# Hybrid mLSTM and attention layer: the mLSTM head norms as steps of their own, and the tanh of the merge gates inside the merge

## The chip, the cores and the metric

The kernel runs on one core of one Trainium2 chip. The metric is the time of one execution in microseconds (us) on the device; lower is better. TensorE (PE in the profile) does the matmuls, VectorE (DVE) and ScalarE (ACT) the elementwise work, GpSimd (POOL) small fills, and SyncE (SP) issues most of the DMA transfers. Each engine works through its own queue strictly in the order in which its instructions stand there.

## The reference, cut to what matters

One layer on a sequence of 512 tokens, width 1024, in float32. Two token mixers, each with four heads of 128 channels, work on the same normed input; each head is normed, and both are merged by gates:

```python
hm = mlstm_chunkwise(heads(mq_c), heads(mk_c), heads(mv), i_pre, f_pre)
hm = head_rmsnorm(hm, m_norm_g)                    # per head, over its 128 channels
ya = (sigmoid(mo) * hm) @ w_br_m

hd = diff_attention(q1, q2, k1, k2, heads(dv), lam, rel_bias)
hd = head_rmsnorm(hd, da_norm_g) * (1.0 - lam_init)
yb = hd @ w_br_d

g_a, g_b = split(gates)
x = x + (sigmoid(g_a) * ya + sigmoid(g_b) * yb) @ w_out
```

Behind it come a gated convolutional feed-forward part (1024 to 2 x 2816 and back), a per-layer embedding and a last norm. The change touches neither the mixers' matmuls nor anything behind the merge.

## The kernel before

Activations lie with channels on the 128 partitions and the 512 tokens in the free dimension. Every large product is taken as three matmuls of high and low parts (`mm3`, L95 to L99: high x high, low x high, high x low), each 128x512. A weight block of 128x1024 is loaded by `wload` (L101) into `raw`, and split on ACT (`whi`, L89) and DVE (`wlo`, L90); there are two buffers each. Projections accumulate in PSUM tiles of the tag `mm`, of which there are four; `sc` and `acc` have two each.

The string ORDER (L50 to L53) is the order in which the code of the mixers is written out. `mq`, `mk`, `dq`, `dk`, `ga`, `gb` are projections, `m0` to `m3` the four mLSTM heads (`mlstm`, L424), `M0` to `M3` their ends (`mlstm_end`, L447), `a0` to `a3` the attention heads (`attention`, L464) and `A0` to `A3` their ends (`attention_end`, L496). A scheduler of the language then sorts the instructions of each engine, by priorities and by its own idea of when operands are ready, so that projections fill the time in which a head waits for ACT and DVE.

What the steps are made of:

- An mLSTM head's sums `num` and `den` grow in PSUM by four blocks. For each, a row `rb` is loaded, taken through Exp on ACT, masked on POOL, multiplied with the scores on DVE (L435) and split (`pph`, `ppl`).
- `mlstm_end` loads a row `em`, and calls `head_norm` (L407). That scales `num` into `y` (L410), squares it into `v` (L412), splits `v` (`csph`, `cspl`), sums it over the partitions with two matmuls into a tile `hm0ss` and so on, and takes the root through `rsqrt_of` (L151): Ln, Exp and Square on ACT (L156 to L158), two operations on DVE (L159, L160), then `y` times `r` (L421). The result is multiplied by the output gate `mo` (L458; its tanh is L444) and split into `hmh` and `hml` (L92, L93).
- `attention_end` calls the same `head_norm` on its sum `av`, with tiles named `hd0ss` and so on, and splits into `hdh` and `hdl`.
- `gate` (L502) is a projection, a multiplication by the token norm `rB` on DVE (L506) and a tanh on ACT (L507). Eight of the sixteen gates stand in ORDER, the others in the merge.
- The merge (L549 to L561) goes over eight chunks of 128 channels. A chunk projects all four `hm` into `ya` and all four `hd` into `yb` (two PSUM tiles of `mm`, 12 matmuls each), multiplies each by its gate (L556, L557), adds them and splits them into `mxh` and `mxl`.

ACT evaluates functions from a loaded table. Ln and Exp of the norms, tanh, and gelu need different tables, and a table load (ACT_TABLE_LOAD) stands wherever the next function isn't in the one that is loaded. `rsqrt_of` is given `before=last`, so that its load is issued right behind the cast of `csph`.

Of the kernel before, what the change touches and what calls it, by code (L numbers as in the profile page):

```python
# [16 lines left out]
P = 128  # L17
# [7 lines left out]
EPS = 1e-6  # L25
# [23 lines left out]

ORDER = """  # L50
bias0 if0 mq0 mk0 mq1 mk1 ct0 m0 m1 mk3 mq2 dk0 M0 M1 mk2 m2 mq3 M2 m3 dq0 dv0 M3 a0 dk1 dq1
A0 a1 A1 dk2 dq2 ga3 dq3 a2 A2 ga0 ga2 gb1 dk3 a3 gb3 gb2 gb0 ga1 A3
"""  # L53


# [1 line left out]
def trunk_kernel(ctx, tc, xT, pT, par, oneh, relb, lamv, w_if, w_in, w_v, w_br, w_out, w_up,  # L57
# [12 lines left out]
    def rt(tag, name):  # L70
        return big.tile([P, S], F32R, tag=tag, name=name, bufs=NBUF[tag])

    def tt(tag, name, n=S):
        w = S + 4 if tag == "ev" else S
        return tp.tile([P, w], F32, tag=tag, name=name, bufs=TBUF[tag])[:, :n]
# [7 lines left out]
    def f(ap):  # L83
        return ap.bitcast(F32)


    def split(hi, lo, src, scale=None):
        if scale is None:
            nc.scalar.copy(hi, src)  # L89
            nc.vector.tensor_sub(lo, src, f(hi))  # L90
        else:
            nc.scalar.activation(hi, src, AF.Copy, scale=scale)  # L92
            nc.vector.scalar_tensor_tensor(lo, src, scale, f(hi), op0=ALU.mult, op1=ALU.subtract)  # L93
# [7 lines left out]
    def wload(src, n=1024):  # L101
        raw = wp.tile([P, 1024], F32, tag="raw", name="raw", bufs=2)
        hi = wp.tile([P, 1024], F32R, tag="whi", name="whi", bufs=2)
        lo = wp.tile([P, 1024], F32R, tag="wlo", name="wlo", bufs=2)
        with tc.high_priority(offset=180):
            nc.sync.dma_start(raw[:, :n], src)
            split(hi[:, :n], lo[:, :n], raw[:, :n])
        return hi, lo
# [25 lines left out]
    def col(c):  # L134
        return prm[:, c:c + 1]
# [7 lines left out]
    def sumsq_add(acc, src, first):  # L143
        if first:
            nc.scalar.activation(acc, src, AF.Square)
        else:
            q = tt("hn", "sq")
            nc.scalar.activation(q, src, AF.Square)
            nc.vector.tensor_add(acc, acc, q)

    def rsqrt_of(r, v, a, before=None):  # L151

        if before is not None:
            with tc.issue_after(before.ins):
                nc.scalar.preload_act_table_set("natural_log_exp_and_others")
        nc.scalar.activation(r, v, AF.Ln, scale=2.0 ** -LN_SHIFT)  # L156
        nc.scalar.activation(r, r, AF.Exp, scale=-0.5, bias=lnb)
        nc.scalar.activation(a, r, AF.Square)  # L158
        nc.vector.scalar_tensor_tensor(a, v, -0.5, a, op0=ALU.mult, op1=ALU.mult)  # L159
        nc.vector.scalar_tensor_tensor(r, a, 1.5, r, op0=ALU.add, op1=ALU.mult)  # L160

    def colsum(o, src):
        hi, lo = pair("cs")
        last = nc.scalar.copy(hi, src)
        nc.vector.tensor_sub(lo, src, f(hi))
        nc.tensor.matmul(o, lhsT=ones, rhs=hi, start=True, stop=False)
        nc.tensor.matmul(o, lhsT=ones, rhs=lo, start=False, stop=True)
        return last
# [235 lines left out]
            nc.tensor.matmul(o, lhsT=ones, rhs=ph, start=j == 0, stop=False)  # L404
            nc.tensor.matmul(o, lhsT=ones, rhs=pl, start=False, stop=j == NB - 1)

    def head_norm(o, g, name, extra=None):  # L407

        y = tt("hn", "y")
        nc.scalar.activation(y, o, AF.Copy, scale=col(g))  # L410
        v = tt("hn", "v")
        nc.scalar.activation(v, o, AF.Square)  # L412
        ss = ps("sc", name + "ss")
        last = colsum(ss, v)
        if extra is None:
            nc.vector.tensor_scalar(v, ss, 1.0 / P, EPS, op0=ALU.mult, op1=ALU.add)
        else:
            nc.vector.scalar_tensor_tensor(v, ss, 1.0 / P, extra, op0=ALU.mult, op1=ALU.add)
        r = tt("hn", "r")
        rsqrt_of(r, v, ss, last)  # L420
        nc.vector.tensor_mul(y, y, r)  # L421
        return y

    def mlstm(hh):  # L424
        num, den = ps("acc", f"num{hh}"), ps("acc", f"den{hh}")
# [19 lines left out]
        return t  # L445

    def mlstm_end(hh, num, den, t):  # L447
        em = tt("rb", "em")
        nc.sync.dma_start(em, rd[hh, ROW_OFF[4]:].partition_broadcast(P))
        nc.scalar.activation(em, em, AF.Exp)  # L450
        ad = tt("hn", "ad")
        nc.scalar.activation(ad, den, AF.Abs)
        nc.vector.tensor_max(em, ad, em)
        nc.scalar.activation(em, em, AF.Square, scale=EPS ** 0.5)
        y = head_norm(num, C_GM + hh, f"hm{hh}", em)
        if t is None:
            t = out_gate(hh)
        nc.vector.scalar_tensor_tensor(y, t, 1.0, y, op0=ALU.add, op1=ALU.mult)  # L458
        hi, lo = rt("hz", f"hmh{hh}"), rt("hz", f"hml{hh}")
        split(hi, lo, y, 0.5)  # L460
        return hi, lo


# [30 lines left out]
        return o  # L494

    def attention_end(hh, o):  # L496
        y = head_norm(o, C_GD + hh, f"hd{hh}")
        hi, lo = rt("hz", f"hdh{hh}"), rt("hz", f"hdl{hh}")
        split(hi, lo, y, 1.0 - LAM_INIT)
        return hi, lo  # L500

    def gate(c, name):  # L502
        o = ps("mm", name)
        proj(o, win(c), 0, h)
        t = tt("x", name)
        nc.vector.tensor_mul(t, o, rB)  # L506
        nc.scalar.activation(t, t, AF.Tanh, scale=0.5)  # L507
        return t


# [2 lines left out]
    for step in ORDER.split():  # L513
        what, i = step[:-1], int(step[-1])
        if what == "if":
            rd, cols = gates()
        elif what == "ct":
            ct = turn_cols(cols)
        elif what == "mq":
            mq[i] = conv_silu(i, 0.5, f"mq{i}")  # L520
        elif what == "mk":
            mk[i] = conv_silu(4 + i, 0.5 * P ** -0.5, f"mk{i}")
        elif what == "mo":
            mo[i] = out_gate(i)
        elif what == "m":
            sums[i] = mlstm(i)
        elif what == "M":
            hm[i] = mlstm_end(i, *sums[i], mo.get(i))
        elif what == "dv":
            dv = vproj(1, "dv")  # L530
        elif what == "bias":
            bias, nlam = make_bias(), make_nlam()
        elif what == "dq":
            dq[i] = queries(8 + i, f"dq{i}")
        elif what == "dk":
            dk[i] = keys(12 + i, f"dk{i}")
# [12 lines left out]
    for j in range(KD):  # L549
        ta = ga[j] if j in ga else gate(20 + j, "ga")  # L550
        tb = gb[j] if j in gb else gate(28 + j, "gb")
        w = wload(w_br[j])
        oa, ob = ps("mm", "ya"), ps("mm", "yb")
        proj(oa, w, 0, hm)
        proj(ob, w, 4, hd)
        nc.vector.scalar_tensor_tensor(ta, ta, 1.0, oa, op0=ALU.add, op1=ALU.mult)  # L556
        nc.vector.scalar_tensor_tensor(tb, tb, 1.0, ob, op0=ALU.add, op1=ALU.mult)  # L557
        nc.vector.tensor_add(ta, ta, tb)
        hi, lo = rt("v", f"mxh{j}"), rt("v", f"mxl{j}")
        split(hi, lo, ta, 0.5)  # L560
        mixed.append((hi, lo))  # L561
# [290 lines left out]
```

## Time and profile before

| | us |
|---|---|
| median of 3 runs (830.2 to 831.01) | 830.45 |
| the profiled execution, its own time | 831.68 |
| its span, first to last instruction | 830.0 |
| PE busy in the span | 813.1 (98%) |
| DVE busy | 541.2 (65%) |
| ACT busy | 412.5 (50%) |
| POOL busy | 28.9 (3%) |
| mean granted TensorE clock | 0.995 of full speed |

Matmuls overlap: a 128x512 matmul is shown as 0.39 us long while the next starts 0.23 us later, so waits on PE are read from the distance between starts, and from the idle time that a row shows in brackets with the instruction that ended it.

### The profile page before, as it was taken

How to read it: one execution, taken by the hardware profiler on the slowest of the kernel's cores; microseconds unless marked ns; L12 is line 12 of the kernel's file. 1: busy time of each engine (PE TensorE's matmuls, PEld its weight loads, DVE VectorE, ACT ScalarE, POOL GpSimd, SP SyncE). 2: the span in 40 equal slices, each digit the busy share in tenths (PEclk: the TensorE clock that was granted, in tenths of full speed). 3: DMA queues.
4: the chain of work that ended last, by engine and by line, in shares of the span. 5: the costliest groups of instructions: out<-in, count | busy, mean ns of one | idle time of the engine just before them, and what ended most of it. 6: DMA issues, size and time to landing. Idle time of an engine off the chain costs nothing.

```text
span 830.0 us, 9910 instructions
## 1 busy us (share of the span) xinstructions
PE 813.1 (98%) x3665; PEld 666.0 (80%) x3665; DVE 541.2 (65%) x875; ACT 412.5 (50%) x624; POOL 28.9 (3%) x117
## 2 busy tenths in 40 slices
PE   9999999999999999999999999999999999999995
PEld 7777778887878888888788888888888888888884
DVE  7698787699767854456677777777777343343546
ACT  7556877687776433234654444444444432232433
POOL 0111100000000000000000000000000000000000
PEclk9999999999999999999999999999999999999998
DMA  6472333222122233352333222333223323333402
GB/s 223 136 207 96 102 109 109 78 77 71 58 76 77 77 102 102 123 181 92 111 103 102 101 82 97 102 108 120 87 92 101 96 89 99 94 112 96 142 36 77
DMA packets 28425, 85.97 MB, mean 104 GB/s; under 512 B 3462, under 2 KB 5146, under 8 KB 28248
## 3 DMA queue, kind: packets, MB, share of 16 engines
q1 hardware_dynamic: 27256, 81.96, 30.9%
q0 software_dynamic: 832, 3.11, 1.3%
q8 instruction: 29, 0.48, 0.2%
q10 hardware_dynamic: 288, 0.27, 0.1%
q14 instruction: 20, 0.16, 0.1%
HBM read 83.19 MB, written 3.45 MB: 104 GB/s over the span
## 4 chain that ended last, share of the span: by engine, by line
PE 85%; ACT 5%; DMA 4%; DVE 4%; issue 1%; POOL 0%; SPq 0%; POOLq 0%; DVEq 0%; ACTq 0%
PE uv L99 5%; PE wd L98 5%; PE wd L99 5%; PE uv L97 5%; PE uv L98 5%; PE wd L97 5%; PE ug L99 5%; PE ug L97 5%; PE ug L98 5%; PE gb L98 2%; PE gb L97 2%; PE gb L99 2%; PE ga L97 2%; PE ga L99 2%; PE ga L98 2%; PE wo L97 2%
## 5 line engine op out<-in xcount | busy, mean ns | idle before, releaser
L89 ACT CAST whi<-raw 128x1024 fp32r<-128x1024 f32 (+1 forms) x137 | 138.3, 1010 | 206.4 <-issue 73.0
L90 DVE TENSOR_TENSOR wlo<-raw,whi 128x1024 fp32r<-128x1024 f32 (+1 forms) x136 | 159.8, 1176 | 87.2 <-ACT whi L89 85.8
L97 PE MATMUL wd<-gh,whi 128*128 128x512 f32 x176 | 68.5, 389 | 0.0
L98 PE MATMUL wd<-gl,whi 128*128 128x512 f32 x176 | 68.5, 389 | 0.0
L99 PE MATMUL wd<-gh,wlo 128*128 128x512 f32 x176 | 68.5, 389 | 0.0
L588 DVE SCALAR_TENSOR_TENSOR y<-u,prm,y 128x512 f32<-128x512 f32 x88 | 65.6, 749 | 1.5
L89 ACT CAST gh<-y 128x512 fp32r<-128x512 f32 x22 | 13.7, 621 | 55.5 <-DVE y L597 55.5
L583 DVE TENSOR_TENSOR u<-uv,rffn 128x512 f32<-128x512 f32 x22 | 15.2, 692 | 38.2 <-PE uv L99 38.2
L97 PEld LDWEIGHTS wd<-gh,whi 128*128 128x128 f32 x176 | 33.0, 188 | 6.9
L98 PEld LDWEIGHTS wd<-gl,whi 128*128 128x128 f32 x176 | 33.0, 188 | 6.9
L99 PEld LDWEIGHTS wd<-gh,wlo 128*128 128x128 f32 x176 | 33.0, 188 | 6.8
L586 ACT ACTIVATE y<-u,prm 128x512 f32<-128x512 f32 x44 | 35.7, 814 | 0.2
L595 ACT ACTIVATE y<-y 128x512 f32<-128x512 f32 x22 | 13.9, 632 | 38.9 <-DVE y L588 38.9
L97 PE MATMUL wo<-mxh,whi 128*128 128x512 f32 x64 | 24.9, 389 | 0.0
L98 PE MATMUL wo<-mxl,whi 128*128 128x512 f32 x64 | 24.9, 389 | 0.0
L99 PE MATMUL wo<-mxh,wlo 128*128 128x512 f32 x64 | 24.9, 389 | 0.0
L90 DVE TENSOR_TENSOR gl<-y,gh 128x512 fp32r<-128x512 f32 x22 | 15.2, 692 | 14.7 <-ACT gh L89 14.7
L481 ACT ACTIVATE e<-e,mx 128x128 f32<-128x128 f32 (+3 forms) x32 | 17.8, 558 | 7.0 <-DVE mx L480 6.8
L210 DVE SCALAR_TENSOR_TENSOR y<-u,prm,y 128x512 f32<-128x512 f32 x24 | 17.8, 743 | 2.1 <-ACT y L208 2.0
L582 POOL MEMSET u<- 128x2 f32 x44 | 4.3, 99 | 366.6 <-DVE y L588 357.2
L571 DVE TENSOR_TENSOR x<-x,wo 128x512 f32<-128x512 f32 x8 | 5.5, 687 | 17.2 <-PE wo L99 17.2
L477 DVE CUSTOM_DVE_ANT_0 e<-ds,bias 128x128 f32<-128x128 f32 (+3 forms) x32 | 15.1, 482 | 2.3 <-PE ds L473 2.2
(1093 smaller groups left out, 2226.7 us busy)
## 6 DMA issues: line engine op xcount, KB each, us to landing
raw<-in_w_up SPq DMA_DIRECT2D x44, 512.0 KB, 3.3
raw<-in_w_in SPq DMA_DIRECT2D x36, 512.0 KB, 3.4
raw<-in_w_down SPq DMA_DIRECT2D x16, 512.0 KB, 3.6
x<-in_xT SPq DMA_DIRECT2D x16, 256.0 KB, 4.5
raw<-in_w_br SPq DMA_DIRECT2D x8, 512.0 KB, 3.2
raw<-in_w_out SPq DMA_DIRECT2D x8, 512.0 KB, 3.8
raw<-in_w_gate SPq DMA_DIRECT2D x8, 512.0 KB, 3.4
raw<-in_w_down SPq DMA_DIRECT2D x8, 384.0 KB, 3.3
```

Source lines behind the costliest of these rows:

```text
L89: nc.scalar.copy(hi, src)
L90: nc.vector.tensor_sub(lo, src, f(hi))
L97: nc.tensor.matmul(o, lhsT=lh, rhs=rh, start=start, stop=False)
L98: nc.tensor.matmul(o, lhsT=lh, rhs=rl, start=False, stop=False)
L99: nc.tensor.matmul(o, lhsT=ll, rhs=rh, start=False, stop=stop)
L210: nc.vector.scalar_tensor_tensor(y, u[:, i:i + S], col(c0 + i), y, op0=ALU.mult, op1=ALU.add)
L477: nc.vector.tensor_tensor_reduce(out=e, in0=s[:, :n], in1=bias[hh][:, S - n:], scale=0.125, scalar=-3.0e38, op0=ALU.add, op1=ALU.max, accu ...
L481: nc.scalar.activation(e, e, AF.Exp, bias=mx[:, 1:2], accum_out=mx[:, 2:3])
L583: nc.vector.tensor_mul(u[:, 2:514], o, rB)
L586: nc.scalar.activation(y, u[:, 2:514], AF.Identity, scale=col(c0 + 2), bias=col(c0 + 3))
L588: nc.vector.scalar_tensor_tensor(y, u[:, i:i + S], col(c0 + i), y, op0=ALU.mult, op1=ALU.add)
L595: nc.scalar.activation(gt, gt, AF.Gelu_apprx_tanh)
```

## The change

`head_norm` is gone. `mlstm_end` keeps the scaling, the square, the column sum and the multiplication by the output gate, and returns `y` and `v`, which now lie in two buffers of the tag `hz`. What is left, from Ln to the split, becomes a step `mlstm_norm`, written `N0` to `N3` in ORDER, among the attention heads. `rsqrt_of` is called there without `before`; of the attention ends only that of head 0 still passes it. The tanh of all sixteen gates moves from `gate` into the merge, and `tc.issue_after(last_exp.ins)` holds each of them behind the last Exp of the norms, that of A3. `last_exp` is a new variable that `rsqrt_of` sets.

```diff
 ORDER = """
-A0 a1 A1 dk2 dq2 ga3 dq3 a2 A2 ga0 ga2 gb1 dk3 a3 gb3 gb2 gb0 ga1 A3
+A0 a1 N0 A1 dk2 dq2 N1 ga3 dq3 a2 N2 A2 ga0 ga2 gb1 dk3 N3 a3 gb3 gb2 gb0 ga1 A3
 """
...
-    def head_norm(o, g, name, extra=None):
-
-        y = tt("hn", "y")
-        nc.scalar.activation(y, o, AF.Copy, scale=col(g))
-        v = tt("hn", "v")
+    def mean_square(o, v, name):
+
         nc.scalar.activation(v, o, AF.Square)
         ss = ps("sc", name + "ss")
-        last = colsum(ss, v)
...
+        return ss, colsum(ss, v)
...
     def mlstm_end(hh, num, den, t):
...
-        y = head_norm(num, C_GM + hh, f"hm{hh}", em)
+        y, v = f(rt("hz", f"hmy{hh}")), f(rt("hz", f"hmv{hh}"))
+        nc.scalar.activation(y, num, AF.Copy, scale=col(C_GM + hh))
+        ss, _ = mean_square(num, v, f"hm{hh}")
+        nc.vector.scalar_tensor_tensor(v, ss, 1.0 / P, em, op0=ALU.mult, op1=ALU.add)
         if t is None:
             t = out_gate(hh)
         nc.vector.scalar_tensor_tensor(y, t, 1.0, y, op0=ALU.add, op1=ALU.mult)
+        return y, v
+
+    def mlstm_norm(hh, y, v):
+        r, t = tt("hn", "r"), tt("hn", "t")
+        rsqrt_of(r, v, t)
+        nc.vector.tensor_mul(t, y, r)
         hi, lo = rt("hz", f"hmh{hh}"), rt("hz", f"hml{hh}")
-        split(hi, lo, y, 0.5)
+        split(hi, lo, t, 0.5)
         return hi, lo
...
     def attention_end(hh, o):
-        y = head_norm(o, C_GD + hh, f"hd{hh}")
+        y, v, r = tt("hn", "y"), tt("hn", "v"), tt("hn", "r")
+        nc.scalar.activation(y, o, AF.Copy, scale=col(C_GD + hh))
+        ss, last = mean_square(o, v, f"hd{hh}")
+        nc.vector.tensor_scalar(v, ss, 1.0 / P, EPS, op0=ALU.mult, op1=ALU.add)
+        rsqrt_of(r, v, ss, None if hh else last)
+        nc.vector.tensor_mul(y, y, r)
...
     def gate(c, name):
...
         nc.vector.tensor_mul(t, o, rB)
-        nc.scalar.activation(t, t, AF.Tanh, scale=0.5)
         return t
...
     for j in range(KD):
         ta = ga[j] if j in ga else gate(20 + j, "ga")
         tb = gb[j] if j in gb else gate(28 + j, "gb")
+        with tc.issue_after(last_exp.ins):
+            for t in (ta, tb):
+                nc.scalar.activation(t, t, AF.Tanh, scale=0.5)
```

The scheduler then puts the engines' instructions in another order. The first place is the end of attention head 3 on PE, from the last matmul of `av3` to the first of the column sum `hd3ss`. `ga` is the last gate projection, `ya` a chunk of the merge. Before:

```order
L99 MATMUL av3_2523<-aph_2559,dvl3_1539 128x256
L99 MATMUL ga_2670<-h5h_231,wlo_2673 128x512
L97 MATMUL ga_2670<-h6h_255,whi_2672 128x512
L98 MATMUL ga_2670<-h6l_256,whi_2672 128x512
L99 MATMUL ga_2670<-h6h_255,wlo_2673 128x512
L97 MATMUL ga_2670<-h7h_282,whi_2672 128x512
L98 MATMUL ga_2670<-h7l_283,whi_2672 128x512
L99 MATMUL ga_2670<-h7h_282,wlo_2673 128x512
L97 MATMUL ya_2734<-hmh0_985,whi_2729 128x512
L98 MATMUL ya_2734<-hml0_986,whi_2729 128x512
L166 MATMUL hd3ss_2708<-csph_2709,ones_89 128x512
```

The same place on PE in the changed kernel, where `ya_2766` is the second chunk of the merge and whi_2761 its weights:

```order
L99 MATMUL av3_2517<-aph_2553,dvl3_1503 128x256
L99 MATMUL ya_2766<-hmh0_1926,wlo_2762 128x512
L97 MATMUL ya_2766<-hmh1_2045,whi_2761 128x512
L98 MATMUL ya_2766<-hml1_2046,whi_2761 128x512
L99 MATMUL ya_2766<-hmh1_2045,wlo_2762 128x512
L97 MATMUL ya_2766<-hmh2_2254,whi_2761 128x512
L98 MATMUL ya_2766<-hml2_2255,whi_2761 128x512
L99 MATMUL ya_2766<-hmh2_2254,wlo_2762 128x512
L97 MATMUL ya_2766<-hmh3_2433,whi_2761 128x512
L98 MATMUL ya_2766<-hml3_2434,whi_2761 128x512
L169 MATMUL hd3ss_2699<-csph_2700,ones_89 128x512
```

The gate projection and the first chunk now stand ahead of this place. From the last matmul of `av3` to the first that reads `hdh3` there stood 43 matmuls before; there stand 21 now.

The second place is ACT in the same stretch, from the scaling of `av3` to the split of head 3. `r` is the tile of Ln and Exp. Before:

```order
L410 ACTIVATE y_2704<-av3_2523,prm_72 128x512
L412 ACTIVATE v_2706<-av3_2523 128x512
L164 CAST csph_2709<-v_2706 128x512
L89 CAST whi_2768<-raw_2767 128x1024
L507 ACTIVATE ga_2701<-ga_2701 128x512
L155 ACT_TABLE_LOAD
L156 ACTIVATE r_2716<-v_2706 128x512
L157 ACTIVATE r_2716<-r_2716,lnb_91 128x512
L158 ACTIVATE hd3ss_2708<-r_2716 128x512
L92 ACTIVATE hdh3_2724<-y_2704 128x512
```

ACT in the changed kernel, from the last Exp (L160) on; L562 is the tanh of the gates:

```order
L160 ACTIVATE r_2696<-r_2696,lnb_91 128x512
L562 ACT_TABLE_LOAD
L562 ACTIVATE ga_2312<-ga_2312 128x512
L161 ACTIVATE hd3ss_2699<-r_2696 128x512
L562 ACTIVATE gb_2659<-gb_2659 128x512
L562 ACTIVATE ga_2692<-ga_2692 128x512
L562 ACTIVATE gb_2378<-gb_2378 128x512
L562 ACTIVATE ga_2345<-ga_2345 128x512
L562 ACTIVATE gb_2626<-gb_2626 128x512
L562 ACTIVATE ga_2080<-ga_2080 128x512
L92 ACTIVATE hdh3_2713<-y_2694 128x512
```

The table load moved from ahead of Ln to behind Exp, and seven tanh came in between Exp and the split; behind the split stands the eighth.

The third place is ACT in the end of mLSTM head 1, from the cast of `csph` on. Before:

```order
L164 CAST csph_1001<-v_998 128x512
L155 ACT_TABLE_LOAD
L89 CAST whi_1250<-raw_1249 128x1024
L92 ACTIVATE hmh0_985<-y_930 128x512
L156 ACTIVATE r_1008<-v_998 128x512
L444 ACT_TABLE_LOAD
L444 ACTIVATE mo_1047<-mo_1047 128x512
L157 ACTIVATE r_1008<-r_1008,lnb_91 128x512
L208 ACTIVATE y_1089<-u_1086,prm_72 128x512
L158 ACTIVATE hm1ss_1000<-r_1008 128x512
```

The same place in the changed kernel:

```order
L167 CAST csph_989<-hmv1_985 128x512
L215 ACTIVATE u_864<-y_867 128x512
L447 ACTIVATE em_977<-em_977 128x512
L89 CAST whi_1033<-raw_1032 128x1024
L92 ACTIVATE mq2h_874<-y_867 128x512
L436 ACTIVATE mo_973<-mo_973 128x512
L422 ACTIVATE rb_1096<-rb_1096,ct_634 128x384
```

No root and no table load is left there. In the whole program 20 table loads stood on ACT before, and 7 stand there now.

## Rows read from the trace of the kernel before

**Rows 1.** The page's first part: busy time, share of the span, instructions.
```profile
PE 813.1 (98%) x3665; PEld 666.0 (80%) x3665; DVE 541.2 (65%) x875; ACT 412.5 (50%) x624; POOL 28.9 (3%) x117
```

**Rows 2.** Windows: stretch, length, busy time by engine (instructions), granted clock, DMA.
```profile
63.70:67.00 3.30, 3.30 (x10) 2.72 (x10) 3.30 (x6) 0.62 (x1) 0.06 (x1) 0.50 0.00 0
87.00:92.00 5.00, 3.56 (x19) 2.67 (x18) 3.76 (x8) 4.60 (x9) 0.29 (x1) 1.00 0.44 82
100.00:160.00 60.00, 58.93 (x272) 47.90 (x272) 44.62 (x69) 44.80 (x71) 3.94 (x14) 1.00 0.32 103
160.00:276.40 116.40, 116.10 (x550) 93.31 (x550) 95.36 (x251) 86.04 (x163) 3.67 (x15) 1.00 0.22 73
276.40:800.00 523.60, 523.49 (x2315) 432.59 (x2314) 303.82 (x383) 208.11 (x266) 6.21 (x44) 1.00 0.32 103
```

**Rows 3.** PE's waits in all: for whom, us in total, times, longest.
```profile
PE num L97 <- ACT pph L89: 2.5, 4, 1.4
PE s L97 <- ACT mk0h L92: 2.0, 1, 2.0
```

**Rows 4.** Timeline of PE, mLSTM heads: start, length, instruction [idle, who ended it].
```profile
106.17 0.39 PE L98 MATMUL mk<-h6l,whi 128*128 128x512 f32 x1
106.77 0.50 PE L166 MATMUL hm1ss<-csph,ones 128*128 128x512 f32 x1 [0.22 <-ACT csph L164]
...
130.14 0.39 PE L97 MATMUL dvp<-whi,h0h 128*128 128x512 f32 x1
130.99 0.36 PE L97 MATMUL num<-pph,mvh 128*128 128x256 f32 x1 [0.46 <-ACT pph L89]
...
147.04 0.39 PE L99 MATMUL dvp<-whi,h3l 128*128 128x512 f32 x1
147.74 0.35 PE L97 MATMUL num<-pph,mvh 128*128 128x256 f32 x1 [0.31 <-ACT pph L89]
```

**Rows 5.** Groups of ACT by line: table loads, count, busy us, mean ns.
```profile
L155 ACT ACT_TABLE_LOAD x10 | 12.8, 1283 | 0.2
```

**Rows 6.** Timeline of PE, end of attention head 3 and start of the merge.
```profile
267.28 0.28 PE L99 MATMUL av<-aph,dvl 128*128 128x256 f32 x1
...
270.72 0.39 PE L167 MATMUL hd3ss<-cspl,ones 128*128 128x512 f32 x1
...
277.09 0.62 PE L97 MATMUL yb<-hdh,whi 128*128 128x512 f32 x2
```

**Rows 7.** Timeline of ACT in the same stretch.
```profile
267.60 0.69 ACT L410 ACTIVATE y<-av,prm 128x512 f32<-128x512 f32 x1 [1.36 <-PE av L99]
268.18 0.59 ACT L412 ACTIVATE v<-av 128x512 f32<-128x512 f32 x1
268.80 0.62 ACT L164 CAST csph<-v 128x512 fp32r<-128x512 f32 x1
...
270.93 1.28 ACT L155 ACT_TABLE_LOAD   x1
272.27 0.63 ACT L156 ACTIVATE r<-v 128x512 f32<-128x512 f32 x1
272.94 0.72 ACT L157 ACTIVATE r<-r,lnb 128x512 f32<-128x512 f32 x1
273.69 0.60 ACT L158 ACTIVATE hd3ss<-r 128x512 f32<-128x512 f32 x1
276.51 0.63 ACT L92 ACTIVATE hdh<-y 128x512 fp32r<-128x512 f32 x1 [2.21 <-DVE y L421]
```

**Rows 8.** Timeline of DVE in the same stretch.
```profile
271.56 0.68 DVE L416 TENSOR_SCALAR v<-hd3ss 128x512 f32<-128x512 f32 x1
...
274.33 0.70 DVE L159 SCALAR_TENSOR_TENSOR hd3ss<-v,hd3ss 128x512 f32<-128x512 f32 x1 [1.11 <-ACT hd3ss L158]
275.06 0.69 DVE L160 SCALAR_TENSOR_TENSOR r<-hd3ss,r 128x512 f32<-128x512 f32 x1
275.78 0.69 DVE L421 TENSOR_TENSOR y<-y,r 128x512 f32<-128x512 f32 x1
```

More of the change, by code (lines that the diff above doesn't have):

```diff
@@ L149, in sumsq_add @@
             nc.vector.tensor_add(acc, acc, q)
+    last_exp = None
     def rsqrt_of(r, v, a, before=None):
@@ L156, in rsqrt_of @@
         nc.scalar.activation(r, v, AF.Ln, scale=2.0 ** -LN_SHIFT)
-        nc.scalar.activation(r, r, AF.Exp, scale=-0.5, bias=lnb)
+        nonlocal last_exp
+        last_exp = nc.scalar.activation(r, r, AF.Exp, scale=-0.5, bias=lnb)
         nc.scalar.activation(a, r, AF.Square)
@@ L405, in weighted @@
             nc.tensor.matmul(o, lhsT=ones, rhs=pl, start=False, stop=j == NB - 1)
-    def head_norm(o, g, name, extra=None):
-        y = tt("hn", "y")
-        nc.scalar.activation(y, o, AF.Copy, scale=col(g))
-        v = tt("hn", "v")
+    def mean_square(o, v, name):
         nc.scalar.activation(v, o, AF.Square)
         ss = ps("sc", name + "ss")
-        last = colsum(ss, v)
[L415 to L422, printed above, removed]
+        return ss, colsum(ss, v)
     def mlstm(hh):
@@ L528, in trunk_kernel @@
             hm[i] = mlstm_end(i, *sums[i], mo.get(i))
+        elif what == "N":
+            hm[i] = mlstm_norm(i, *hm[i])
         elif what == "dv":
```

## The prediction

> **What bounds the kernel now.** I read the page's first part first: PE is busy 98% of the span, the other engines 65% or less [rows 1]. So the sum is PE's own work plus the stretches in which PE waits, and a change that takes nothing off PE can win only those. The windows say where they are. From 160 us to 276.4 us PE is busy 116.10 of 116.40 us, and behind that 523.49 of 523.60; from 100 us to 160 us, where the mLSTM heads 1 to 3 end, it is 58.93 of 60.00 [rows 2]. The busy time hides small losses, because matmuls overlap, so I took the pace: 2315 matmuls in 523.60 us are 0.226 us each [rows 2]. Against that pace, the distances between starts hold 0.60 - 0.23 = 0.37, 0.85 - 0.23 = 0.62 and 0.70 - 0.23 = 0.47 us of waiting [rows 4]. That is 1.46 us in all, and each time ACT ends the wait. The list of waits shows the rest of what ACT costs: 2.5 us in four waits for `pph`, the longest 1.4 us, and 2.0 us once for `mk0h` [rows 3]. The longest of both kinds lie ahead of the column sum `hm0ss`, and up to there no engine's order is changed. What the change can win is therefore small.
>
> The last thing to read is the handover from attention head 3 to the merge, since ACT's order was changed most there. The last matmul of `av3` starts at 267.28, and the first that reads `hdh3` is the second of the pair at 277.09, so it starts near 277.3 [rows 6]. The chain between them runs over ACT and DVE and ends with the split at 276.51 + 0.63 = 277.14 [rows 7]. PE has 43 other matmuls queued in between, 43 x 0.226 = 9.7 us, and the chain takes 9.86 us from 267.28 on. The two are equal within 0.2 us: PE doesn't wait, but it has nothing to spare.
>
> **What is removed.** A table load takes 1283 ns [rows 5], and the next function starts 1.34 us after the load did (270.93 to 272.27) [rows 7]. 13 of 20 loads go, 13 x 1.34 = 17.4 us of ACT. ACT isn't the bound, so this counts only where PE waits for ACT. In `M1` to `M3` the loads, Ln, Exp, Square and the split of each head leave ACT's queue, and `pph` no longer stands behind them or behind `em`. I take the 1.46 us as won [rows 4].
>
> **What is moved into the attention.** Each `N` step issues four operations on ACT (Ln, Exp, Square, split; 0.60 to 0.72 us) and four on DVE (0.69 us) [rows 7, 8]. Head 3's stood inside the stretch 160 to 276.4 already, so it gets twelve more of each: on DVE 12 x 0.69 = 8.3 us on top of 95.36, 103.7 of 116.4 us or 89% [rows 2]. ACT gets 12 x 0.65 = 7.8 us, and loses six of the eight loads that lay there, 6 x 1.34 = 8.0, so it stays at 86. Both engines have room; the cover is PE's queue of projections. If DVE doesn't keep up, PE waits at the transposes and at `av`, which is a rival below. No transfer is added and SP's queue keeps its kinds of work. But the heads 2 and 3 of the mLSTM now stand closer together on PE, with less projection work between the end of `hm2ss` and the third block of `num3`, whose row waits for the buffer that `em` frees. Such a wait costs between 0 and the longest, 1.4 us [rows 3]; I take 0.8, between the 0.47 us that this place has now [rows 4] and that longest. So the mixers up to `av3` come out at -1.46 + 0.8 = -0.7 us.
>
> **What is moved into the merge.** Here the change adds a wait. The order shows three facts. PE has 21 matmuls, not 43, between the last of `av3` and the first that reads `hdh3`: the last gate and the first merge chunk have been used up earlier, because the attention of the heads 2 and 3, slowed by the `N` steps, stands later among them. Behind these 21 there is nothing else, since the third chunk needs a PSUM tile and a pair of weight buffers of the first one, and the first one needs `hdh3`. And ACT now has a table load and seven tanh between the last Exp and the split that makes `hdh3`.
>
> I walk the chain from the start of the last `av3` matmul, with the lengths of ACT and DVE [rows 7, 8]. As before, `csph` is cast by 268.80 + 0.62 - 267.28 = 2.14 us. Then `cspl` on DVE 0.68 (taken as `v` of DVE) to 2.86, its matmul 0.39 [rows 6] to 3.3, `v` 0.68 to 4.0, Ln 0.67 to its successor, and Exp 0.72 to 5.44. The load takes 1.28, to 6.74. The first tanh starts at 6.76. Operations of ACT that wait for nothing follow each other at 0.58 us (267.60 to 268.18) [rows 7]: Square starts at 7.34, six tanh follow, and the split starts at 7.34 + 7 x 0.58 = 11.40 and ends at 12.03. DVE is done earlier: from Square's end at 7.94 it has three operations of 0.70 and one gate product, until 10.9, so the tanh and not DVE decide. PE has run dry at 0.11 + 21 x 0.226 = 4.86. **PE waits 12.05 - 4.86 = 7.2 us.**
>
> The wait has a tail. The next matmul needs `hdl3`, one DVE operation later (0.69), 0.5 us more than PE's pace. The third chunk's weights share buffers with the first chunk's, so their split can only start when PE has read the first's last block; that adds some 0.4 us for the high part and 0.5 for the low part, by the same rows. At full pace the tail is 1.4 us. The clock makes it longer: behind the 2.0 us wait for `mk0h` [rows 3] the granted clock was 0.50, the lower of its two levels (1.2 of 2.4 GHz), for the 3.3 us of the window 63.70 to 67.00, in which 10 matmuls started [rows 2]. A wait of 7.2 us is longer than that one, so I expect the same behind it. Nine matmuls stand before PE needs the low weights; at half pace they take 9 x 0.43 + 0.3 for `hdl3` = 4.2 us instead of 2.0. The tail is then 2.1 us, and the waits for weights fall into it. The merge start costs 7.2 + 2.1 = **9.3 us**, at least 7.2 + 1.4 = 8.6 if the clock stays up.
>
> **Sum.** 9.3 - 0.7 = 8.6 us. On the profiled execution this is 831.68 + 8.6 = 840.3. That execution lies 1.2 us above the median of the runs, so on the median 830.45 + 8.6 = **839.0 us**. Nothing behind the merge gives it back: from 276.4 to 800 PE has 0.1 us of idle time [rows 2].
>
> **The rivals.** *The ACT queue was what PE waited for, and the handover stays hidden (faster).* Then the relieved ACT gives back those 1.46 us [rows 4] and the 0.30 us of the attention [rows 2], and the `av3` chain fits behind PE's queue: 830.45 - 1.46 - 0.30 = 828.7. It decides where the chain from `av3` to `hdh3` is shorter than 4.86 us. For it speaks that all of these waits end on ACT; against it, that the part of the chain up to the end of Exp is 5.4 us alone, with no tanh in it. 4%. In the Trainium skill, "ScalarE: Activation LUTs", section "What ACT_TABLE_LOAD costs", a switch of tables is put at 1283 ns plus a drain of about 1380 ns, 2.66 us, and the section on table sets advises to batch calls by set. By that rule ACT sheds 13 x 2.66 = 34.6 us, an estimate from the page, and this rival would be the likely one. The trace agrees on the load and not on the drain: Ln started 0.06 us behind the load's end [rows 7]. And the batching is what puts the seven tanh in front of `hdh3`, which the rule doesn't weigh.
>
> *Nothing measurable.* The wait at the merge is there but is only some 1 to 2 us, because PE arrives late from waits that it had anyway: 830.45 +- 1.7. Against it: every such wait would itself add to the time. 4%.
>
> *The wait without its tail.* The clock stays up, and all 1.46 us are won with no new wait: 8.6 - 1.46 = 7.1, or 837.6; with two of the tail's waits gone as well (0.9 us), 836.7. For it: behind the 1.4 us wait [rows 3] the granted clock stayed at 1.00, the window 87 to 92 us [rows 2]. 22%.
>
> *DVE becomes the bound of the attention.* At 89% busy and in strict order, a part of its 8.3 us more comes through to PE at the scores, transposes and `av`. If a third does, 839.0 + 2.8 = 841.8; if half, 843.2. For it: the scheduler moved the scores of the heads 2 and 3 later, as if DVE were full. Against it: PE's waits in 160 to 276.4 are 0.3 us now [rows 2], and where scores stand later, projections stand in front of them as cover. 17%.
>
> **How the numbers follow.** The forecast 839.0 has 53%. With 22% at 836.7 to 837.6 and 17% at 841.8 to 843.2, the range is 834.5 to 843.5 and leaves out the two rivals of 4% and some of the ends. Its low end takes the 7.2 us with only the 0.5 for `hdl3` as tail, all of the 1.46 and 0.30 us won (836.4), 0.1 us less at each of the 14 steps of the walk, and half of the spread of the runs, 0.4. The high end is the fourth rival's 843.2 with the same 0.4. Slower by over 0.2%, about what a measurement of this kernel can tell from no change (1.7 us): 92%. Within it 4%, faster 4%.
>
> **What would show it.** In the profile of the changed kernel, a wait on PE of about 7 us at the first `yb` that reads `hdh`, put down to ACT `hdh` L92, near 275 us. Behind it some 3 us of a granted clock of 0.5, and matmuls 0.43 us apart. On ACT, the row of tanh in front of that split. Between 100 and 160 us PE's waits for `csph` and `pph` of the old places gone, and perhaps one near 0.8 us at the third block of `num3`. From 160 us to `av3`, DVE near 89% with PE still near 100%. I am wrong if PE doesn't wait at `hdh3`, if the wait is much shorter than 7 us, or if waits of more than 2 us appear at `at` or `av`.

## The result and the profile of the changed kernel

The changed kernel takes 840.28 us (median of 4 runs, 839.08 to 841.12), the kernel before 830.73 beside it: a ratio of 1.0108, 95% interval 1.0087 to 1.0129, or 9.5 us more. Forecast were 839.0 us, with a range of 834.5 to 843.5. The span of the profiled execution is 838.9 us (830.0 before), its own time 840.65. One of the runs below, of `norms_early_tanh_behind`, took 1657.06 us, twice its others, and is left out.

First the page's busy line and four windows of the changed kernel (stretch, length, busy time by engine with instructions, granted clock, DMA), which answer to [rows 1] and [rows 2]:

```profile
PE 815.0 (97%) x3665; PEld 666.2 (79%) x3665; DVE 541.4 (65%) x875; ACT 395.1 (47%) x611; POOL 30.9 (4%) x117
```

```profile
100.00:160.00 60.00, 59.05 (x274) 48.17 (x273) 36.70 (x55) 31.48 (x51) 4.02 (x13) 1.00 0.29 101
160.00:276.40 116.40, 116.08 (x550) 92.61 (x549) 98.41 (x257) 76.19 (x156) 3.72 (x15) 1.00 0.21 73
276.40:800.00 523.60, 517.03 (x2269) 426.52 (x2268) 305.44 (x386) 212.62 (x274) 6.21 (x44) 0.99 0.31 103
281.80:291.90 10.10, 6.42 (x14) 4.67 (x15) 7.82 (x12) 6.88 (x11) 0.00 (x0) 0.50 0.15 48
```

ACT is busy 17.4 us less, and the time is 9.5 us longer. The counts on PE say where: from 100 to 160 us it starts 2 matmuls more than before (0.45 us won), from 160 to 276.4 the same 550, and behind that 2269 instead of 2315. These 46 overstate the loss, since some of them, near 800 us, are short. A better measure is the first matmul behind the merge, that of `wo`, ahead of which both kernels have 1583 matmuls. The kernel before:

```profile
357.04 0.39 PE L97 MATMUL wo<-mxh,whi 128*128 128x512 f32 x1
```

and the changed kernel:

```profile
366.31 0.39 PE L97 MATMUL wo<-mxh,whi 128*128 128x512 f32 x1
```

It comes 9.3 us later, although PE was 0.45 us ahead when the merge began, so the start of the merge costs 9.7 us. The last row of the windows, with 14 matmuls in 10 us at half the clock, lies in this stretch. PE's list of waits (for whom, us in total, times, longest) has one new large entry:

```profile
PE yb L97 <- ACT hdh L92: 6.5, 1, 6.5
PE num L97 <- ACT pph L89: 2.7, 4, 1.5
PE s L97 <- ACT mk0h L92: 1.9, 1, 1.9
...
PE rmixss L169 <- ACT csph L167: 1.0, 1, 1.0
```

The timeline of PE around that wait (start, length, instruction, idle time ahead of it) answers to [rows 6]:

```profile
273.77 0.28 PE L99 MATMUL av<-aph,dvl 128*128 128x256 f32 x1
...
278.63 0.39 PE L99 MATMUL yb<-hdh,wlo 128*128 128x512 f32 x1
285.48 0.79 PE L97 MATMUL yb<-hdh,whi 128*128 128x512 f32 x1 [6.46 <-ACT hdh L92]
286.21 0.79 PE L98 MATMUL yb<-hdl,whi 128*128 128x512 f32 x1
286.80 0.63 PE L99 MATMUL yb<-hdh,wlo 128*128 128x512 f32 x1
287.23 0.63 PE L97 MATMUL yb<-hdh,whi 128*128 128x512 f32 x1
```

Between 273.77 and 278.63 PE works off its 21 matmuls, then it has nothing until 285.48: a distance of 6.85 us where 0.23 would be its pace, so 6.6 us. Behind it the starts are 0.43 us apart. ACT (answering to [rows 7]) shows what it does meanwhile:

```profile
277.95 0.63 ACT L158 ACTIVATE r<-v 128x512 f32<-128x512 f32 x1 [2.04 <-DVE v L502]
278.61 0.72 ACT L160 ACTIVATE r<-r,lnb 128x512 f32<-128x512 f32 x1
279.35 1.28 ACT L562 ACT_TABLE_LOAD   x1
280.65 0.63 ACT L562 ACTIVATE ga<-ga 128x512 f32<-128x512 f32 x1
281.18 0.58 ACT L161 ACTIVATE hd3ss<-r 128x512 f32<-128x512 f32 x1
281.70 0.61 ACT L562 ACTIVATE gb<-gb 128x512 f32<-128x512 f32 x1
...
284.30 0.61 ACT L562 ACTIVATE ga<-ga 128x512 f32<-128x512 f32 x1
284.82 0.61 ACT L92 ACTIVATE hdh<-y 128x512 fp32r<-128x512 f32 x1
```

The load and one tanh stand ahead of Square, six more tanh, 0.52 us apart, ahead of the split. DVE (answering to [rows 8]) has its last operation on the way at 283.84:

```profile
283.84 0.68 DVE L504 TENSOR_TENSOR y<-y,r 128x512 f32<-128x512 f32 x1
```

It ends at 284.52, 0.3 us before the split starts: the tanh decide, but by little.

### The profile page after: what moved, and what is told of

It is laid out like the page before. It is cut to its first block, busy times and chain, and to the rows that moved or that the text cites. A ratio compares the mean times of both kernels' runs of the same rounds, so it can differ in the third digit from the quotient of the medians.

```text
span 838.9 us, 9892 instructions
## 1 busy us (share of the span) xinstructions
PE 815.0 (97%) x3665; PEld 666.2 (79%) x3665; DVE 541.4 (65%) x875; ACT 395.1 (47%) x611; POOL 30.9 (4%) x117
## 4 chain that ended last, share of the span: by engine, by line
PE 87%; DVE 4%; DMA 3%; ACT 3%; issue 2%; SPq 0%; POOL 0%; POOLq 0%; DVEq 0%; ACTq 0%
PE wd L99 5%; PE wd L97 5%; PE uv L97 5%; PE uv L98 5%; PE uv L99 5%; PE wd L98 5%; PE ug L98 5%; PE ug L97 5%; PE ug L99 5%; PE ga L97 2%; PE ga L99 2%; PE ga L98 2%; PE gb L99 2%; PE gb L98 2%; PE gb L97 2%
## 5 line engine op out<-in xcount | busy, mean ns | idle before, releaser
L97 PE MATMUL yb<-hdh,whi 128*128 128x512 f32 x32 | 13.4, 418 | 6.5 <-ACT hdh L92 6.5
```

What stands on the lines that cost most here:

```text
L97: nc.tensor.matmul(o, lhsT=lh, rhs=rh, start=start, stop=False)
```

## The experiments

Each kernel is compared with runs of the kernel before taken beside it, whose median was 830.7 to 831.7 us. "Last start" and "first of `hdh3`" are distances on PE from the start of the last `av3` matmul; the wait is that of PE's list. "Matmuls between" are those on PE between the last of `av3` and the first that reads `hdh3`.

| kernel | matmuls between | last start ahead of the wait | first of `hdh3` | wait | median, us |
|---|---|---|---|---|---|
| changed kernel | 21 | 4.87 | 11.72 | 6.5 | 840.28 |
| `tanh_behind_split` | 21 | 4.88 | 9.10 | 3.8 | 838.86 |
| `norm_steps_alone` | 27 | 6.27 | 10.39 | 3.7 | 840.96 |
| `norm3_later` | 29 | 6.73 | 11.73 | 4.6 | 839.61 |
| `dve_load_alone` | 26 | 6.05 | 9.11 | 2.7 | 836.05 |
| `norms_short` | 44 | 10.21 | 11.86 | 1.3 | 833.19 |
| `tanh_move_alone` | 49 | | | none | 832.83 |
| `pe_kept_busy` | 48 | | | none | 837.15 |
| `norms_before_attention` | 55 | | | none | 836.60 |

The fourth column is a chain over ACT and DVE, about 9.1 us without the row of tanh, 11.8 with it, and 10.4 where a load stands ahead of Exp. The third is 0.11 us plus 0.227 for each matmul, within about 0.1 in all six rows. Their difference, less one matmul of 0.23, is the wait within 0.2 us. So the wait has two causes that can be moved one by one: the chain, and the cover on PE, that is, the matmuls it still has to do. In the kernel before the first that reads `hdh3` starts near 277.3 [rows 6], 10.0 us behind `av3`, with 43 matmuls in between and no wait. Of the 6.6 us of the changed kernel, 22 matmuls fewer are 5.0, and the chain, longer by 1.7, is the rest.

### The tanh behind the split of `hdh3`

```diff
-        with tc.issue_after(last_exp.ins):
+        with tc.issue_after(hd3_split.ins):
```

`hd3_split` is the operation on ACT that makes `hdh3`.

> The changed kernel, with the tanh of the merge gates ordered behind the split that makes hdh3 instead of behind the last Exp; PE's order is unchanged, with the same 21 matmuls between av3 and the first that reads hdh3. Theory A (the table load and the seven tanh stand in the chain to hdh3): Square starts 1.83 us earlier (279.35 instead of 281.18 in the trace of the changed kernel), then DVE's three operations of 0.70 us, with or without one gate product between them, decide; the split moves from 284.82 to between 282.0 and 282.7, so the wait at hdh3 falls from 6.5 to between 3.7 and 4.4 us. Some of it comes back, since the load, the tanh and the two weight splits now stand behind hdh3: up to 0.5 us. So 2.1 to 2.8 us less than the changed kernel's 840.3, about 837.5 to 838.2. Theory B (the loss is the lost cover on PE, whatever stands on ACT): as the changed kernel, 840.3. Theory C (the queue of tanh is all of the loss): back to the kernel before, 830.7.

Measured: 838.86 us (836.59 to 839.71), a ratio of 1.0096 (1.0075 to 1.0117). One row of PE's waits and four of ACT:

```profile
PE yb L100 <- ACT hdh L95: 3.8, 1, 3.8
```

```profile
278.80 0.60 ACT L164 ACTIVATE hd3ss<-r 128x512 f32<-128x512 f32 x1
281.61 0.63 ACT L95 ACTIVATE hdh<-y 128x512 fp32r<-128x512 f32 x1 [2.21 <-DVE y L507]
282.26 1.28 ACT L566 ACT_TABLE_LOAD   x1
283.55 0.63 ACT L566 ACTIVATE ga<-ga 128x512 f32<-128x512 f32 x1
```

Without the tanh ACT waits for DVE ahead of the split, and the wait is what theory A gave, 2.7 us shorter. Only 1.4 us of it shows in the median, from runs that lie 3 us apart, and 3.2 us in the spans of the two profiled executions (838.9 and 835.7), so the size of what comes back behind the split isn't settled. The larger part of the loss stays: the tanh row isn't all of it.

### Each half of the change alone

```diff
 A0 a1 A1 dk2 dq2 ga3 dq3 a2 A2 ga0 ga2 gb1 dk3 a3 gb3 gb2 gb0 ga1 A3
...
+        with tc.issue_after(last_exp.ins):
+            for t in (ta, tb):
+                nc.scalar.activation(t, t, AF.Tanh, scale=0.5)
```

> The kernel before with the second half of the change alone: tanh moved into the merge behind the last Exp, norms left at the ends of the mLSTM heads. By the order PE has 49 matmuls between the last of av3 and the first that reads hdh3, and ACT has a load and six tanh ahead of the split. Theory A: PE runs dry at 0.11 + 49 x 0.226 = 11.2 us behind the start of the last av3 matmul. ACT: csph cast until 2.14, load until 3.44, a weight split of 1.05 until 4.5, Ln and Exp until 5.9, load until 7.2, tanh, Square and five tanh at 0.52 us each to 10.8, split until 11.4. The wait is 0.2 to 0.5 us, and the time 830.7 to 831.7. A rival: a load and a row of tanh ahead of the split cost the 6 us that they take on ACT, whatever PE has left to do: 837. Another rival: the moved N steps carry nothing of the loss and this kernel is as slow as the changed one, 840.

Measured: 832.83 us, a ratio of 1.0028 (1.0016 to 1.0041). There is no wait for `hdh3` in PE's list; its largest entries are those of the kernel before:

```profile
PE num L97 <- ACT pph L89: 2.7, 4, 1.6
PE s L97 <- ACT mk0h L92: 1.8, 1, 1.8
```

The row of tanh, behind which PE waited 6.5 us, costs nothing at the handover when 49 matmuls cover it; both rivals fall. The 2.0 us that it is slower lie elsewhere: in its trace PE has lost them when the projection `if` starts, at 32.1 us instead of 30.1. The order of no engine differs up to there.

```diff
         nc.vector.tensor_mul(t, o, rB)
+        nc.scalar.activation(t, t, AF.Tanh, scale=0.5)
         return t
...
-        with tc.issue_after(last_exp.ins):
-            for t in (ta, tb):
-                nc.scalar.activation(t, t, AF.Tanh, scale=0.5)
```

> The changed kernel with the first half of the change alone: the norms as steps of their own in the attention, tanh back in the gates. By the order PE has 27 matmuls between the last of av3 and the first that reads hdh3; no tanh stands between Exp and the split, but a load stands ahead of Ln and another ahead of Exp in every norm (15 loads in all). Theory A: PE runs dry at 0.11 + 27 x 0.226 = 6.2 us. ACT: csph until 2.14, load until 3.44, Ln at 4.0 to 4.7, load to 6.0, Exp to 6.7, Square to 7.3; DVE three operations of 0.70 to 9.4; split to 10.0. The wait is 3.8 us, with a tail of 1.4 to 3 us behind it and 0.7 us won in the mixers: 835.2 to 836.8. Rival: the moved norms are harmless and the tanh row is all of the loss: 830.

Measured: 840.96 us, a ratio of 1.0124 (1.0109 to 1.0139). The wait at `hdh3` is what was expected, but theory A missed the time by 4 us, since new waits on DVE stand in the attention:

```profile
PE yb L97 <- ACT hdh L92: 3.7, 1, 3.7
...
PE at L494 <- DVE mx L479: 1.2, 1, 1.2
PE ds L475 <- DVE mx L479: 0.8, 2, 0.6
PE ds L475 <- DVE r L163: 0.5, 1, 0.5
```

In its trace the last `av3` starts 2.1 us later than in the changed kernel (275.84), although 6 matmuls fewer stand ahead of it: that is 3.4 us. So the N steps alone cost as much as the whole change, and the tanh alone 2.0 us, none of it at the handover. The tanh in the merge take the table loads out of the attention (15 loads here, 7 in the changed kernel) and lengthen the chain at its end; together with the N steps that comes out even.

### PE kept busy through the wait

```diff
+    warm2 = ps("acc", "warm2")
+    with tc.issue_after(last_mm.ins):
+        for i in range(28):
+            nc.tensor.matmul(warm2, lhsT=ones, rhs=hm[0][0], start=i == 0, stop=i == 27)
```

`last_mm` is the second matmul of the column sum of head 3, and nothing reads `warm2`.

> The changed kernel with 28 matmuls of 128x512 added that nothing reads, queued on PE behind the column sum of attention head 3, so that PE works through the wait for hdh3 (48 matmuls in between instead of 20 or 21; 28 x 0.226 = 6.3 us, the length of the wait). In the trace of the changed kernel the granted clock is 0.50 for 10.24 us from inside the wait on, and PE's starts from 260 to 300 us hold 11.3 us beyond its pace, 6.6 of them the wait itself. Theory A (the tail is the clock that fell while PE stood still): the clock stays at 1.00, the matmuls behind hdh3 follow at 0.22 us, the wait shrinks to about 0.7 us, and the time falls by 2 to 3 us to 837.3 to 838.3, although PE has 28 matmuls more to do. Rival (the tail is waits for hdl3 and for weights, which a busy PE doesn't shorten): the same time as the changed kernel, 840.3.

Measured: 837.15 us (836.81 to 837.57), 3.1 us less than the changed kernel, with 28 matmuls more. Two windows, from the added matmuls on:

```profile
278.00:284.00 6.00, 6.00 (x28) 4.74 (x26) 3.88 (x6) 5.99 (x11) 0.00 (x0) 1.00 0.00 0
284.00:300.00 16.00, 15.98 (x70) 12.80 (x69) 13.11 (x19) 6.92 (x9) 0.00 (x0) 1.00 0.30 98
```

The granted clock stays at 1.00 and the matmuls at their pace, and no wait for `hdh` is left in PE's list. What stood behind the wait was the clock, and the weights and `hdl3` cost nothing that can be seen beside it.

### A gate held back as cover

```diff
-                ga[i] = gate(20 + i, "ga")
+            with tc.issue_after(last_av.ins) if ("ga", i) in LATE else nullcontext():
+                ga[i] = gate(20 + i, "ga")
```

`LATE` holds `ga1` alone, and `last_av` is the last matmul of the attention sum.

> The changed kernel with the N steps and the tanh where the change puts them, but the projection of the last gate of the order (ga1, 24 matmuls) held back on PE until behind the last matmul of av3. 62 matmuls then stand between it and the first that reads hdh3, 24 of them ahead of the column sum of head 3. Theory A (cover): PE runs dry at 0.11 + 62 x 0.226 = 14.1 us; the column sum comes only behind 24 matmuls, at 5.5 us, which makes the chain some 2.8 us longer than 11.7: 14.5. The wait is about 0.4 us; if the attention, which has lost 24 matmuls to put between its own, still keeps PE at work, the time is 830.5 to 832. Rival (the attention on DVE is as slow as the order assumes, and the N steps are the bound): PE waits in the attention for what it lost, 24 x 0.226 = 5.4 us, and the time is 836 to 838.

Measured: 844.05 us, a ratio of 1.0149 (1.0123 to 1.0175): slower than the changed kernel, and beyond both theories. PE no longer waits at `hdh3`; it waits in attention head 3. Two rows of its waits and the windows around:

```profile
PE at L501 <- DVE e L495: 2.5, 2, 1.3
PE at L501 <- DVE mx L486: 2.5, 1, 2.5
```

```profile
160.00:260.00 100.00, 99.70 (x472) 79.87 (x471) 87.19 (x227) 69.51 (x142) 3.38 (x13) 1.00 0.22 74
260.00:276.00 16.00, 9.59 (x29) 5.91 (x28) 10.59 (x31) 5.37 (x13) 0.34 (x2) 0.62 0.09 33
```

Between the scores, the transposes and `av` of the last head PE now has nothing to do for 6.4 of 16 us, and the clock falls there instead. The rival has the place and the size of the waits (5.4 us), but not the time, 6 us over its 838; how much of that is the clock, no run parts. The projections are one stock: what is kept for the handover is missing in the attention. The same kernel with the tanh behind the split:

> As gate_behind_av3, and the tanh of the merge ordered behind the split that makes hdh3. 52 matmuls in between: PE runs dry at 11.9 us, the chain of 8.9 with the later column sum ends at 11.7. Theory A: no wait at hdh3 and 829.8 to 831, the same as the kernel before. Rival (DVE is the bound in the attention): waits of up to 5.4 us there, 835.

Measured: 843.16 us (1.0141, 1.012 to 1.0163), with the same waits at the transposes. The rival's waits came in both, its 835 didn't, and my own belief, that the attention has projections to spare, fell.

### The norms ahead of the attention

```diff
-A0 a1 N0 A1 dk2 dq2 N1 ga3 dq3 a2 N2 A2 ga0 ga2 gb1 dk3 N3 a3 gb3 gb2 gb0 ga1 A3
+A0 a1 A1 dk2 dq2 ga3 dq3 a2 A2 ga0 ga2 gb1 dk3 a3 gb3 gb2 gb0 ga1 A3
```

and `N0 N1 N2 N3` stand between `M3` and `a0`.

> The changed kernel with its four N steps moved in the order of steps to one place ahead of attention head 0, so that none of them stands in the attention; tanh stays in the merge, behind the last Exp, as in the changed kernel. By the order 55 matmuls stand on PE between the last of av3 and the first that reads hdh3 (the changed kernel has 21, the one before 43), 17 of them ahead of the column sum. Theory A (the loss is the length of the chain to hdh3 minus PE's cover): PE runs dry at 0.11 + 55 x 0.226 = 12.5 us behind the start of the last av3 matmul; the chain is the changed kernel's 11.7 and about 1.1 more, since the column sum comes only after 17 matmuls (3.95 us), 12.8. The wait is 0 to 0.5 us, and the time 830.5 to 832. Rival (the row of tanh and the load cost what they take on ACT, wherever the norms stand): 837. Rival (norms outside the end of the head cost their time on DVE wherever they stand): 839.

Measured: 836.60 us (1.006, 1.0042 to 1.0077). The wait at `hdh3` is gone, as theory A has it, but the time isn't. Two rows of PE's waits and two of DVE's timeline:

```profile
PE mo L97 <- DVE dvl L296: 2.0, 1, 2.0
...
PE ds L475 <- DVE mx L479: 1.5, 1, 1.5
```

```profile
157.59 0.69 DVE L162 SCALAR_TENSOR_TENSOR t<-hmv,t 128x512 f32<-128x512 f32 x1 [2.35 <-ACT t L161]
...
161.87 2.06 DVE L296 SCALAR_TENSOR_TENSOR dvl<-dvp,rtok,dvh 128x512 fp32r<-128x512 f32 x3
```

The norms now stand on DVE ahead of `dvl`, which frees the PSUM tiles that the output gate's projection needs, and DVE waits there for ACT, which has 15 table loads again, eight of them between 139 and 167 us. The price has moved; the two waits are 3.5 of the 5.7 us over the kernel before. With the tanh behind the split as well:

> As norms_before_attention, and the tanh of the merge ordered behind the split that makes hdh3. 45 matmuls in between: PE runs dry at 0.11 + 45 x 0.226 = 10.3 us; the chain without the tanh row took 8.9 by the walk, with the later column sum 10.0. Theory A: no wait at hdh3, 830 to 831, the same as the kernel before within 0.2%; a gain over the kernel before only if the fewer table loads (15 instead of 20) take something off the waits for pph, at most 1 us. Rival: the weights and the gate products, which now stand behind the tanh, make PE wait in the second and third chunk, 1 to 2 us: 831.5 to 833.

Measured: 836.78 us (835.59 to 837.7; 1.0065, 1.0049 to 1.0081), with the same wait of 2.0 us for `dvl` and none at `hdh3`; theory A and the rival both missed that wait.

### Work on DVE alone, and less of it

```diff
+        elif what == "D":
+            d = tt("hn", "d")
+            nc.vector.tensor_mul(d, rB, rB)
+            for _ in range(3):
+                nc.vector.tensor_mul(d, d, rB)
...
-A0 a1 A1 dk2 dq2 ga3 dq3 a2 A2 ga0 ga2 gb1 dk3 a3 gb3 gb2 gb0 ga1 A3
+A0 a1 D0 A1 dk2 dq2 D1 ga3 dq3 a2 D2 A2 ga0 ga2 gb1 dk3 D3 a3 gb3 gb2 gb0 ga1 A3
```

> The kernel before, unchanged but for sixteen products of 128x512 on DVE that nothing reads, in four steps of four at the places of the attention where the change puts its N steps (0.69 us each, 11 us of DVE). No instruction is added on PE or ACT. The order answers with 26 matmuls between the last of av3 and the first that reads hdh3 instead of 43. Theory A (the attention of the kernel before has no slack on DVE: what is put there uses up PE's stock of projections, and PE stands still at the end of it): PE runs dry at 0.11 + 26 x 0.226 = 6.0 us, the chain to hdh3 is the 9.9 us of the kernel before, the wait 3.9 us, with a tail of 2 to 3 us at the lower clock: 836.5 to 838. Rival (DVE, busy 95 of 116 us there, has room for it): 830.7.

Measured: 836.05 us (1.0056, 1.0035 to 1.0076), 4.4 us over the kernel before, with no edit on ACT or PE. A row of PE's waits and the window behind it:

```profile
PE yb L97 <- ACT hdh L92: 2.7, 1, 2.7
```

```profile
282.80:286.10 3.30, 3.03 (x7) 2.03 (x8) 1.45 (x3) 1.56 (x3) 0.00 (x0) 0.50 0.00 0
```

The chain was 0.8 us shorter than I had taken it, and PE ran dry 0.3 us later. The rival falls: with DVE busy 95 of 116 us there [rows 2], 11 us more weren't free, though a part fitted in: from 160 to 268 us DVE is busy 97.7 us, 89.6 before. And the 26 matmuls come from the scheduler's order, which is made ahead of the run by its own idea of DVE; whether DVE itself would have let `av3` come earlier, this run doesn't tell.

```diff
-        rsqrt_of(r, v, t)
+        nc.scalar.activation(r, v, AF.Ln, scale=2.0 ** -LN_SHIFT)
+        nc.scalar.activation(r, r, AF.Exp, scale=-0.5, bias=lnb)
         nc.vector.tensor_mul(t, y, r)
```

> The changed kernel with a shorter N step: the Square on ACT and the two operations on DVE that refine the inverse root of the mLSTM heads are left out, so that a head's step has two operations on DVE instead of four (8 x 0.69 = 5.5 us less on DVE in the attention). The heads' norms come out with the precision of Ln and Exp alone. By the order 44 matmuls stand between av3 and the first that reads hdh3. Theory A: PE runs dry at 0.11 + 44 x 0.226 = 10.1 us, the chain with the tanh row takes 11.7, the wait is 1.6 us and the time 832 to 834. Rival (the tanh row is the loss whatever DVE does): 837 or more.

Measured: 833.19 us (1.0025, 1.0014 to 1.0037). The last `av3` matmul starts at 267.89 us, 5.9 us earlier than in the changed kernel and near the 267.28 of [rows 6], with 44 matmuls behind it; the 23 matmuls that the order no longer puts ahead of it are 5.2 us of that. What is left is the row of tanh alone, in PE's list:

```profile
PE yb L97 <- ACT hdh L92: 1.3, 1, 1.3
```

These two kernels part the causes: less cover alone (26 matmuls for 43) costs 4.4 us, the longer chain with the cover kept 1.5. The whole change loses five more matmuls of cover, 1.1 us, and its longer wait is followed by 14 matmuls at half pace instead of 7, another 1.6 us. That makes 8.6 of the 9.5 us, as a rough estimate: the causes don't simply add, since with short cover the row of tanh is worth 2.7 us of wait (`tanh_behind_split`) and here 1.3.

### One N step later, and the kernel before once more

```diff
-A0 a1 N0 A1 dk2 dq2 N1 ga3 dq3 a2 N2 A2 ga0 ga2 gb1 dk3 N3 a3 gb3 gb2 gb0 ga1 A3
+A0 a1 N0 A1 dk2 dq2 N1 ga3 dq3 a2 N2 A2 ga0 ga2 gb1 dk3 a3 N3 gb3 gb2 gb0 ga1 A3
```

> The changed kernel with the step N3 behind attention head 3 in the order of steps instead of ahead of it. 29 matmuls stand between the last of av3 and the first that reads hdh3 (21 in the changed kernel), and ACT's row of tanh is as there. Theory A: every matmul of cover takes 0.226 us off the wait, which is 11.7 - 0.11 - 29 x 0.226 = 5.0 us instead of 6.5 or 6.8; the tail stays; 1.8 us less than 840.3, 838.5. Rival (the attention, with less to put between its matmuls, waits on DVE for what the cover gains, as it did where a gate was held back): 840.3 and waits at the transposes.

Measured: 839.61 us (838.65 to 840.46). The wait fell to 4.6 us, as theory A has it with 0.4 to spare; the time by 0.7 us instead of 1.8, with runs that overlap those of the changed kernel. Against the kernel before beside it (831.68) it is 7.9 us slower, 1.6 less than the changed kernel's 9.5. By time alone this run decides nothing.

> The kernel before once more, unchanged, with a profile of its own: how far its runs and the waits of its first 65 us spread. Every kernel with an edit has shown 5.6 to 7.4 us beyond PE's pace in the first 60 us, the profile of the kernel before 5.2, though nothing of the change lies there; and a granted clock of 0.50 stood behind the wait for mk0h in that profile and not in that of the changed kernel. If the start varies from run to run, this profile lies somewhere in 5 to 7.4; if it goes with the program, it repeats 5.2 within 0.2. Expected: the former, and a median of 830 to 831.

Measured: 832.21 us (830.08 to 833.4, 10 runs), a ratio of 1.0001 (0.9987 to 1.0014), above the 830 to 831 that I expected. PE waited 1.3 us for the first `whi` (0.4 in the first profile) and lies 5.9 us behind its pace at 60 us, against 5.2. So the start varies from run to run; whether the 2.0 us of `tanh_move_alone` are only that stays open.

## The prediction, step by step

**What bounds the kernel** held: 17.4 us less on ACT brought 0.5 us, and PE's waits decided.

**What is removed** held: 412.5 to 395.1 us of ACT. That it holds to the tenth is luck, since 13 loads of 1.283 us [rows 5] are 16.7 us of busy time, and the rest lies elsewhere in ACT's queue. By the estimate from the Trainium skill, "ScalarE: Activation LUTs", section "What ACT_TABLE_LOAD costs", with its drain, it would have been 34.6. The trace doesn't show that drain: the first tanh starts at 280.65, 0.02 us behind the load's end. The rival that hung on it, a faster kernel, didn't come.

**What is moved into the attention.** The net of -0.7 us for the mixers is about what 2 more matmuls from 100 to 160 us show, 0.5. The new wait at `num3` came, 0.60 us beyond the pace (predicted 0.8), and a second of 0.68 at 122.8 us, which I hadn't seen. DVE is busy 98.4 us from 160 to 276.4, not 103.7: the attention itself has become longer, and its end and gate products lie behind the window. ACT is busy 76.2 us there and not 86: I left out that the tanh of eight gates leave this stretch, 8 x 0.63 = 5.0 us, and a part of head 3's end. The weak step of this part is another. I wrote that both engines have room and kept DVE as a rival that would show as waits in the attention. `dve_load_alone` and `norms_short` show that with DVE's work there `av3` moves, by 6.7 and 5.9 us for 11 and 5.5 us of it; it doesn't show as waits because the order fills PE from its stock of projections, and PE pays at the end, when the stock is gone. That DVE is the limit on the chip too, and not only in the scheduler's idea, is shown for the changed kernel alone, by the waits of `gate_behind_av3`. The 21 matmuls in place of 43 that I read from the order were this effect, so the sum had it, at the other place.

**What is moved into the merge.** The mechanism, the place and the engines were right. The chain was walked to 12.05 us and measured 11.72, since tanh follow each other at 0.52 us and not 0.58; PE could have started the next matmul at 4.87 + 0.23 = 5.10, where I had 4.86. So the wait is 6.6 us for 7.2. The mis-sized term is the tail: the start of the merge cost 9.7 us, 3.1 of them besides the wait, where I had 2.1. I took the length of the low clock from the 3.3 us behind the wait for `mk0h`, and counted nine matmuls at half pace. Here it began inside the wait and lasted to 291.9, 6.4 us behind the wait's end, with 14 matmuls at half pace, some 14 x 0.226 = 3.2 us lost. `pe_kept_busy` gives 3.1 us back, about the whole tail. That 9.3 was predicted and 9.7 lost is in part luck: the wait was 0.6 us too long, the tail 1.0 too short.

**The sum** of 8.6 us stands against 9.5 in the medians and 9.0 in the profiled executions (831.68 to 840.65). A part of both numbers is chance: the clock that had fallen behind `mk0h` before stayed up in the profile of the changed kernel, while PE lost 1.0 us at `rmixss` in the first 25 us. By the time the last block of `num0` starts, at 88.83 us, it is 0.3 us earlier than before (89.16).

**The rivals.** "Hidden handover" and "nothing measurable" are out. "The wait without its tail" fell with the clock. "DVE becomes the bound" named the resource and was wrong about where it is seen; no experiment gave a kernel faster than the one before.

## What to carry to other kernels

An engine that is always busy may live on a stock of independent work; before moving operations onto a neighbour of it, count what is left of the stock where it ends, and measure the slack by adding useless operations there. Batching functions to save table loads puts them ahead of whatever comes next in the same queue, so look at which chain stands behind them. Behind a long wait, look whether the granted clock fell, add the slow stretch to the wait, or give the engine something to do.

## What the runs showed of the hardware

A wait of some 2 us does or doesn't lower PE's clock, and its length alone doesn't say which. Behind the wait for `mk0h` the granted clock fell to 0.50 in the profile of the kernel before [rows 2], and in `dve_load_alone` behind 2.1 us; it stayed at 1.00 in the kernel before run again, where the wait was longer. The window behind it and the wait, in `before_again`, then the window in `dve_load_alone`:

```profile
PE s L97 <- ACT mk0h L92: 2.2, 1, 2.2
```

```profile
63.50:67.00 3.50, 3.25 (x15) 2.65 (x16) 3.23 (x6) 1.46 (x4) 0.14 (x2) 1.00 0.01 5
```

```profile
64.40:67.60 3.20, 3.20 (x10) 2.70 (x9) 3.19 (x6) 0.62 (x1) 0.10 (x1) 0.50 0.00 0
```

PE starts 10 matmuls in 3.2 us there or 15 in 3.5. Between 60 and 80 us it lost 4.8 us against its pace in the first profile of the kernel before and 3.7 in the second, so the same wait costs about 1 us more in one execution than in the next.
